# Down projections by seven products: where a pair's first half stands against the end of the pair before it

## The chip, the cores and the metric

The kernel runs on one core of one Trainium2 chip. The metric is the device time of one execution of the whole program, in microseconds (us), taken as the median of three runs. Engines are named as in the profile: PE is TensorE (matrix products), PEld its weight loads, DVE is VectorE, ACT is ScalarE, SP is SyncE, which issues the loads.

## The reference, cut to what matters

The program is a decoder trunk with two layers on 512 rows of 1024 values, all in float32. The first layer mixes tokens with a gated DeltaNet, the second with sliding-window attention on a shared K/V. Each layer ends with the same gated MLP, and the change lies in its last product only:

```python
def conv_gated_mlp(hn, w_up, conv_w, conv_b, w_down):
    u = causal_dwconv(hn @ w_up, conv_w, conv_b)
    gate, val = jnp.split(u, 2, axis=-1)
    return (jax.nn.silu(gate) * val) @ w_down

# in reference(), for each of the two layers (D_FF = 2816, D_MODEL = 1024)
h = h + conv_gated_mlp(rmsnorm(h, ffn_norm_w[layer]), ffn_w_up[layer],
                       ffn_conv_w[layer], ffn_conv_b[layer], ffn_w_down[layer])
```

## The kernel before, in words

*Layout.* Activations are kept transposed, 128 features on the partitions and the 512 rows along the free axis. A float32 operand is split into a high part (`hi`, rounded by a copy on ACT, L132) and a low part (`lo`, what the rounding left, a subtraction on DVE, L133). Each product of two operands is three matmuls: high by high, high by low, low by high (L1052, L1053 and L1054 here; L162 to L164 in the up projections).

*Up and down in two blocks.* The hidden width of 2816 is 22 tiles of 128. In each layer the kernel makes 12 tiles with an up projection and multiplies them by their rows of `w_down` (a down projection), then the other 10. That makes four down projections: layer 0 with six pairs of hidden tiles, layer 0 with five, layer 1 with six, layer 1 with five. In the profiled execution they lie at 655.7 to 718.8, 827.6 to 881.9, 1174.3 to 1237.2 and 1346.0 to 1386.6 us.

*Seven products.* The 1024 output features are eight tiles of 128, taken in four pairs (`m2` = 0 to 3). A 2 by 2 block of weights (two hidden tiles by two output tiles) times a 2 by 2 block of activations (two hidden tiles by two halves of 256 rows) is made with seven block products instead of eight. `forms()` has prepared the sums of activation blocks (`B11`, `B21`, `T1`, ...); `seven_products()` makes the sums of weight blocks on DVE and runs the products. In the last down projection the last pair of output tiles is done plainly (`last_mm`) and goes with the final normalisation.

*Steps of a pair.* `seven_products` is a generator. Its `yield`s cut a pair into three steps:
- first half (`u` = 0): the products `a` (B11), `b` (B21), `d` (T1) and `c` (T4) over the first three pairs of hidden tiles; 36 matmuls.
- second half (`u` = 1): the same over the remaining two or three pairs, after which DVE adds the four sums to `h`.
- end: T2 and B22 are added up in the banks of `a` and `d` (a `cast` for each half); the block A22 of both halves is rounded into `w4` (`cast_to`, L156 on DVE); DVE adds `a` and `d` to `h`; then the products T3 run from `w4` into `e`, which DVE adds to `h` last. 54 matmuls with six pairs.

*What sets the order.* The order in which the generators are advanced, `(0, 1, 0, 0, 1, 1)` for pairs 0 and 1 and three steps in a row for each later pair, is the order in which the instructions are written down. Below that a scheduler places the instructions on each engine by its own estimates of when operands are ready, so neighbours on DVE can change places. Each engine then runs its list strictly in order and waits by semaphores.

*Weight buffers.* The weights of each half (`sts[u]`, 768 KB for three pairs of hidden tiles) are loaded by SP in `down_stage` (L1034). Two loads of three take a buffer of the tag `stage`, every third one the buffer `st3`; there are three buffers in all. So load number n takes the buffer of load n - 3, and can be issued once that has been read for the last time. For the load of a second half, that is the buffer of the first half of the pair before, whose last reader is the first `cast_to` in that pair's end. DVE also writes the weight sums into these buffers in place (L1063, L1071, L1072, L1080). `whi` and `wlo` have three buffers each, in `cast` and `weights`.

*Banks.* Sums are held in banks of tags `d`, `g`, `s` and `p`: `a` in `d`, `b` in `g`, the product `d` in `s`, `c` in `p` for even pairs and `d` for odd ones, `e` in `g` for even pairs and `p` for odd ones.

## Time and profile before

| what | value |
|---|---|
| times of the three runs | 1419.02, 1417.68, 1416.81 us |
| median | 1417.68 us |
| span of the profiled execution | 1412.6 us (the profile gives no other time of it) |
| busy: PE, PEld | 1384.7 (98%), 1167.1 us (83%) |
| busy: DVE, ACT | 1108.1 (78%), 748.1 us (53%) |
| the four down projections, by the stretches above | 63.1, 54.3, 62.9 and 40.6 us |

The profile is of one execution. A row of the busy times by stretch has the stretch (start:end, in us from the start of the span), its length, and then, for PE, weight loads, DVE, ACT, POOL and SP in this order, the busy time and in brackets the number of instructions; behind them the mean granted TensorE clock (1.00 is full), the busy share of the DMA engines and the GB/s moved. A row of the chain of waits has the start, the time the chain spends there, the engine, what is written (and, of a load, from what) and the line. A row of a timeline has the start, the duration, the engine, the line, the operation, output<-inputs, its size, and in brackets the idle time ahead of it with what ended it. SPq stands for the issue of a DMA on SP's queue.

### The profile page before, as it was taken

The numbers are of one execution on the slowest core, as the hardware profiler recorded it, in microseconds if no ns is written. First come the engines' busy times: TensorE is split into PE (matmuls) and PEld (weight loads), VectorE is DVE, ScalarE is ACT, GpSimd is POOL, SyncE is SP. The second block draws the span as 40 slices with busy tenths as digits, with TensorE's granted clock in tenths as the row PEclk, the third lists the DMA queues.
The fourth block names the chain that finished last, engine by engine and source line by source line (L and its number), as shares of the span: only waits on it lengthen the run. The fifth ranks groups of instructions, "written<-read, shape, count | busy, mean of one in ns | idle before, by whom it ended". The sixth has DMA issues, their size and how long they took to land.

```text
span 1412.6 us, 21751 instructions
## 1 busy us (share of the span) xinstructions
PE 1384.7 (98%) x8370; PEld 1167.1 (83%) x8370; DVE 1108.1 (78%) x2070; ACT 748.1 (53%) x1470; POOL 15.6 (1%) x37
## 2 busy tenths in 40 slices
PE   7999999999999999999999999999999999999998
PEld 5787888878877888888988889777788888988897
DVE  4996896978856438879878889788668888878996
ACT  7764566656658225444344446567544444444543
POOL 1000000000100000000000000000000000000000
PEclk9999999999999999999999999999999999999999
DMA  5333254172465323221443223322132231432222
GB/s 161 92 103 115 79 175 126 61 231 84 140 225 159 119 90 112 90 90 46 135 150 119 75 79 109 109 71 76 61 112 90 90 101 49 146 106 82 92 75 75
DMA packets 162299, 151.80 MB, mean 107 GB/s; under 512 B 24148, under 2 KB 150677, under 8 KB 162197
## 3 DMA queue, kind: packets, MB, share of 16 engines
q1 hardware_dynamic: 159938, 150.22, 33.2%
q8 instruction: 66, 1.08, 0.3%
q10 hardware_dynamic: 2259, 0.20, 0.1%
q14 instruction: 36, 0.29, 0.1%
HBM read 133.60 MB, written 15.75 MB: 106 GB/s over the span
## 4 chain that ended last, share of the span: by engine, by line
PE 87%; DVE 6%; DMA 2%; ACT 2%; issue 1%; SPq 0%; DVEq 0%; ACTq 0%
PE d L162 20%; PE d L163 20%; PE d L164 20%; PE g L198 2%; DVE wlo L133 2%; PE d L1054 1%; PE d L1207 1%; PE d L1211 1%; PE d L1209 1%; PE d L1052 1%; PE d L1053 1%; PE s L1054 1%; PE s L1052 1%; PE s L1053 1%; PE s L659 1%
## 5 line engine op out<-in xcount | busy, mean ns | idle before, releaser
L162 PE MATMUL d<-xh,whi 128*128 128x512 f32 x1128 | 444.2, 394 | 0.2
L163 PE MATMUL d<-xl,whi 128*128 128x512 f32 x1128 | 444.0, 394 | 0.0
L164 PE MATMUL d<-xh,wlo 128*128 128x512 f32 x1128 | 441.9, 393 | 0.3 <-DVE wlo L156 0.3
L132 ACT CAST whi<-stage 128x1024 fp32r<-128x1024 f32 (+2 forms) x234 | 227.4, 976 | 247.7 <-PE d L163 165.1
L133 DVE TENSOR_TENSOR wlo<-stage,whi 128x1024 fp32r<-128x1024 f32 (+2 forms) x234 | 263.4, 1128 | 70.4 <-ACT whi L132 69.6
L162 PEld LDWEIGHTS d<-xh,whi 128*128 128x128 f32 x1128 | 211.7, 188 | 44.9 <-ACT xh L172 0.5
L164 PEld LDWEIGHTS d<-xh,wlo 128*128 128x128 f32 x1128 | 211.6, 188 | 44.6 <-DVE wlo L156 0.7
L163 PEld LDWEIGHTS d<-xl,whi 128*128 128x128 f32 x1128 | 211.7, 188 | 43.2 <-issue 0.5
L280 DVE SCALAR_TENSOR_TENSOR acc<-d,cwc,acc 128x511 f32<-128x511 f32 (+2 forms) x96 | 70.7, 739 | 8.7 <-ACT acc L277 7.9
L913 DVE TENSOR_TENSOR sz<-d,p6s 128x512 f32<-128x512 f32 x59 | 40.6, 688 | 42.9 <-PE d L164 40.7
L935 ACT ACTIVATE dt<-dt 128x512 f32<-128x512 f32 x44 | 27.8, 631 | 78.3 <-DVE dt L918 78.3
L918 DVE SCALAR_TENSOR_TENSOR dt<-sz,fcw,dt 128x511 f32<-128x511 f32 (+1 forms) x60 | 44.8, 747 | 1.8 <-ACT dt L916 0.9
L918 DVE SCALAR_TENSOR_TENSOR va<-sz,fcw,va 128x511 f32<-128x511 f32 (+1 forms) x58 | 43.3, 747 | 0.9
L561 DVE TENSOR_TENSOR sT<-sT,p6s 64x31 f32<-64x31 f32 (+15 forms) x124 | 40.9, 330 | 2.0
L555 DVE TENSOR_TENSOR p6s<-sN,sT 64x31 f32<-64x31 f32 (+15 forms) x124 | 40.7, 328 | 1.9
L1276 ACT ACTIVATE dt<-dt,sm 128x256 f32<-128x256 f32 (+1 forms) x64 | 30.1, 471 | 21.5 <-DVE sm L1259 21.5
L132 ACT CAST whi<-st 128x768 fp32r<-128x768 f32 (+1 forms) x30 | 23.7, 792 | 30.5 <-PE g L1053 9.0
L913 DVE TENSOR_TENSOR zl<-d,p6s 128x512 f32<-128x512 f32 x29 | 20.0, 688 | 17.8 <-PE d L164 17.8
L682 ACT ACTIVATE rq<-o 128x128 f32<-128x128 f32 x64 | 19.0, 301 | 25.4 <-DVE o L677 22.3
L937 DVE TENSOR_TENSOR va<-dt,va 128x512 f32<-128x512 f32 x44 | 30.4, 690 | 1.2
L133 DVE TENSOR_TENSOR wlo<-st,whi 128x768 fp32r<-128x768 f32 (+1 forms) x30 | 26.8, 899 | 2.2 <-ACT whi L132 2.2
L916 ACT ACTIVATE dt<-sz,normc,fcw 128x512 f32<-128x512 f32 x30 | 24.5, 815 | 6.5 <-DVE sz L913 6.0
(770 smaller groups left out, 2876.2 us busy)
## 6 DMA issues: line engine op xcount, KB each, us to landing
stage<-in_ffn_w_up_dram SPq DMA_DIRECT2D x44, 1024.0 KB, 4.8
stage<-in_a_w_in_dram SPq DMA_DIRECT2D x23, 1024.0 KB, 5.8
stage<-in_ffn_w_down_dram SPq DMA_DIRECT2D x16, 768.0 KB, 4.3
stage<-in_a_w_out_dram SPq DMA_DIRECT2D x8, 1024.0 KB, 5.0
st<-in_ffn_w_down_dram SPq DMA_DIRECT2D x8, 768.0 KB, 5.3
zd<-sz SPq DMA_DIRECT2D x16, 256.0 KB, 2.6
od<-o SPq DMA_DIRECT2D x16, 256.0 KB
stage<-in_b_w_q_dram SPq DMA_DIRECT2D x4, 1024.0 KB, 5.0
```

The costliest lines, as they stand in the source:

```text
L132: S.copy(hi[:, :kt, :m], src)
L133: V.tensor_tensor(lo[:, :kt, :m], src, hi[:, :kt, :m].bitcast(F32), op=ALU.subtract)
L162: PE.matmul(ps, hi[:, k, :m], xh[k], start=first and k == 0, stop=False)
L163: PE.matmul(ps, hi[:, k, :m], xl[k][:], start=False, stop=False)
L164: done.append(PE.matmul(ps, lo[:, k, :m], xh[k], start=False, stop=last and k == kt - 1))
L280: V.scalar_tensor_tensor(acc[:, d:], ps[:, : T - d], col, acc[:, d:], op0=ALU.mult, op1=ALU.add)
L555: V.tensor_tensor(tv, N[:, s, s + 1 : 32].unsqueeze(2).to_broadcast([64, n, m]), Tm[:, s : s + 1, 0:m].to_broadcast([64, n, m]), op=ALU.mult,)
L561: V.tensor_tensor(Tm[:, s + 1 : 32, 0:m], Tm[:, s + 1 : 32, 0:m], tv, op=ALU.subtract)
L913: V.tensor_tensor(u[:], ps[:], rs[:], op=ALU.mult)
L918: V.scalar_tensor_tensor(acc[:, d:], u[:, : T - d], tap(2 - d, t), acc[:, d:], op0=ALU.mult, op1=ALU.add)
L937: V.tensor_tensor(b[:], a[:], b[:], op=ALU.mult)
L1276: S.activation(ej, ej, AF.Exp, bias=ngm[:, i : i + 1], scale=-1.0, accum_out=den[:, i : i + 1])
```

## The change

The order of the steps changes; in pairs (m2) and steps (first half F, second half S, end E):

```
before   0F 1F 0S 0E 1S 1E 2F 2S 2E 3F 3S 3E
after    0F 1F 0S 0E 1S 2F 1E 2S 3F 2E 3S 3E
last down projection (three pairs by seven products)
before   0F 1F 0S 0E 1S 1E 2F 2S 2E
after    0F 1F 0S 0E 1S 2F 1E 2S 2E
```

The first half of pair 1 stands where it stood. The first halves of pairs 2 and 3 now stand ahead of the end of the pair before. The sum `e` takes a bank of tag `g` in all pairs. No instruction is added or dropped, and SP issues the loads in the same order as before.

```diff
--- before.py
+++ after.py
@@ -945,14 +945,14 @@
                 sts = [down_stage(src) for src in srcs]
                 if not (plain and m2 == KD // 2 - 1):
                     todo.append(seven_products(sts, srcs, parts, sevens, h_pairs[m2], m2 % 2))
-
                     if m2 == 1:
-                        for i in (0, 1, 0, 0, 1, 1):
-                            next(todo[i])
+                        advance(todo, "0 1 0")
                     elif m2 > 1:
-                        for _ in range(3):
-                            next(todo[m2])
+                        advance(todo, f"{m2 - 2} {m2 - 1} {m2} ")
+                    if m2 == KD // 2 - 1:
+                        advance(todo, f"{m2 - 1} {m2} {m2}")
                     continue
+                advance(todo, f"{m2 - 2} {m2 - 1} {m2 - 1}")
                 xs2 = [x for f in sevens for x in (f["f0"], f["f1"])]
 
                 def last_mm(ps, ws, ts, u):
@@ -1021,6 +1021,10 @@
         out.update(halves(("T1", "T2"), parts(ta[:], next(rows), next(rows))))
         out.update(halves(("T3", "T4"), parts(tb[:], next(rows), next(rows))))
         return out
+
+    def advance(todo, order):
+        for i in order.split():
+            next(todo[int(i)])
 
     turns = [0]
 
@@ -1079,7 +1083,7 @@
                 add(h21, c)
             V.tensor_tensor(A22, A22, A11, op=ALU.subtract)
             yield
-        e = bank("p" if odd else "g")[:, 0:256]
+        e = bank("g")[:, 0:256]
         w4 = weights()
         for u in range(2):
             w = cast(sts[u], 2 * len(parts[u]), 0)
```

In the changed kernel the lines from the new function on are numbered four higher: L1052 to L1054 become L1056 to L1058, L1057 becomes L1061, L1063 L1067, L1071 L1075, L1072 L1076, L1080 L1084.

The lists of DVE in the first down projection show the three places that the prediction speaks of. `h4` and `pz` are output tiles, into which a sum of a bank (`d`, `g`, `s`, `p`) is added; `stage` and `st3` are weight buffers, in which weight sums are made in place; `whi` and `wlo` are the high and low parts.

The first place is DVE behind the last read of the buffer that the load for pair 2's second half takes. Before (the first row is that read, from `st3_995`; the first use of the load, into `st3_1036`, stands two rows behind the last one shown):

```order
L156 TENSOR_TENSOR wlo_1030_6469<-st3_995_6183,whi_1029_6468 128x384
L1057 TENSOR_TENSOR h4_4550<-h4_4550,d_1008_6242 128x256
L156 TENSOR_TENSOR wlo_1030_6469<-stage_996_6185,whi_1029_6468 128x384
L133 TENSOR_TENSOR wlo_1034_6495<-stage_996_6185,whi_1033_6494 128x768
L1063 TENSOR_TENSOR stage_1035_6539<-stage_1035_6539 128x3x128
L133 TENSOR_TENSOR wlo_1042_6549<-stage_1035_6539,whi_1041_6548 128x768
L1057 TENSOR_TENSOR h4_4550<-h4_4550,d_1005_6239 128x768
L1071 TENSOR_TENSOR stage_1035_6539<-stage_1035_6539 128x3x128
L1057 TENSOR_TENSOR h4_4550<-h4_4550,s_1007_6241 128x256
L1072 TENSOR_TENSOR stage_1035_6539<-stage_1035_6539 128x3x128
L133 TENSOR_TENSOR wlo_1044_6573<-stage_1035_6539,whi_1043_6572 128x768
L1057 TENSOR_TENSOR h4_4550<-h4_4550,p_1028_6467 128x512
```

After (the first row is the read, the last one the first use of the load, now called `st3_1018`):

```order
L156 TENSOR_TENSOR wlo_1042_6529<-st3_995_6183,whi_1041_6528 128x384
L156 TENSOR_TENSOR wlo_1042_6529<-stage_996_6185,whi_1041_6528 128x384
L133 TENSOR_TENSOR wlo_1046_6555<-stage_996_6185,whi_1045_6554 128x768
L1061 TENSOR_TENSOR h4_4550<-h4_4550,d_1005_6239 128x768
L1061 TENSOR_TENSOR h4_4550<-h4_4550,s_1007_6241 128x256
L1067 TENSOR_TENSOR st3_1018_6345<-st3_1018_6345 128x3x128
```

Before, the sums and casts of a whole first half (`stage_1035`) stand between the two; now only the rest of pair 1's end stands there, two low parts and two additions.

The second place is what follows on DVE. Before, from that first use on, with pair 3's first half in `stage_1056`:

```order
L1063 TENSOR_TENSOR st3_1036_6541<-st3_1036_6541 128x3x128
L133 TENSOR_TENSOR wlo_1046_6597<-st3_1036_6541,whi_1045_6596 128x768
L1063 TENSOR_TENSOR stage_1056_6719<-stage_1056_6719 128x3x128
L1071 TENSOR_TENSOR st3_1036_6541<-st3_1036_6541 128x3x128
L133 TENSOR_TENSOR wlo_1048_6623<-st3_1036_6541,whi_1047_6622 128x768
```

After, with pair 3's first half in `stage_1038`:

```order
L1067 TENSOR_TENSOR st3_1018_6345<-st3_1018_6345 128x3x128
L133 TENSOR_TENSOR wlo_1048_6601<-st3_1018_6345,whi_1047_6600 128x768
L133 TENSOR_TENSOR wlo_1050_6627<-st3_1018_6345,whi_1049_6626 128x768
L1061 TENSOR_TENSOR h4_4550<-h4_4550,g_1040_6527 128x512
L1061 TENSOR_TENSOR pz_728_4551<-pz_728_4551,d_1030_6471 128x256
L1075 TENSOR_TENSOR st3_1018_6345<-st3_1018_6345 128x3x128
L1061 TENSOR_TENSOR pz_728_4551<-pz_728_4551,g_1031_6472 128x256
L1076 TENSOR_TENSOR st3_1018_6345<-st3_1018_6345 128x3x128
L1084 TENSOR_TENSOR st3_1018_6345<-st3_1018_6345 128x3x128
L1061 TENSOR_TENSOR pz_728_4551<-pz_728_4551,s_1032_6473 128x256
L1067 TENSOR_TENSOR stage_1038_6523<-stage_1038_6523 128x3x128
L1061 TENSOR_TENSOR pz_728_4551<-pz_728_4551,p_1033_6474 128x256
```

The first weight sum of pair 3's first half (L1063 on `stage_1056`, now L1067 on `stage_1038`), which the second of its two casts reads, stood two rows behind; now it stands ten rows behind, after two low parts, the last addition of pair 1 (`h4` from `g_1040`), three additions of pair 2 (`pz_728`) and three weight sums.

The third place is the end of the first down projection, where the next up projection's first weights (`stage_1077`) are split. Before:

```order
L1057 TENSOR_TENSOR pz_729_4552<-pz_729_4552,d_1058_6723 128x768
L1057 TENSOR_TENSOR pz_729_4552<-pz_729_4552,s_1060_6725 128x256
L133 TENSOR_TENSOR wlo_1080_6904<-stage_1077_6899,whi_1079_6903 128x1024
L1057 TENSOR_TENSOR pz_729_4552<-pz_729_4552,p_1070_6827 128x512
L133 TENSOR_TENSOR wlo_1085_6940<-stage_1078_6901,whi_1084_6939 128x1024
```

After:

```order
L1061 TENSOR_TENSOR pz_729_4552<-pz_729_4552,d_1051_6651 128x768
L1061 TENSOR_TENSOR pz_729_4552<-pz_729_4552,s_1053_6653 128x256
L1061 TENSOR_TENSOR pz_729_4552<-pz_729_4552,g_1070_6827 128x512
L133 TENSOR_TENSOR wlo_1080_6904<-stage_1077_6899,whi_1079_6903 128x1024
L133 TENSOR_TENSOR wlo_1085_6940<-stage_1078_6901,whi_1084_6939 128x1024
```

The addition of pair 3's `e` (`p_1070` before, `g_1070` now) and the low part from `stage_1077` have changed places.

## The prediction

> I call the four down projections D1 to D4 in the order in which they run, the pairs of output tiles 0 to 3 (`m2`), and the three steps of a pair H0, H1 and E (first half, second half, end). All times are microseconds (us).

> **What bounds the kernel now.** I read the page first, then the busy times by stage, then the chain of waits, then the two queues that feed these stages.

> ```profile
> PE 1384.7 (98%) x8370; PEld 1167.1 (83%) x8370; DVE 1108.1 (78%) x2070; ACT 748.1 (53%) x1470; POOL 15.6 (1%) x37
> PE 87%; DVE 6%; DMA 2%; ACT 2%; issue 1%; SPq 0%; DVEq 0%; ACTq 0%
> stage<-in_ffn_w_down_dram SPq DMA_DIRECT2D x16, 768.0 KB, 4.3
> ```

> TensorE (PE) bounds the program: 98% of the span and 87% of the chain. So the change can only win what TensorE stands still in D1 to D4. The busy times of D1 to D4, in this order, with the number of matmuls in brackets behind each:

> ```profile
> 655.70:718.80 63.10, 61.96 (x506) 60.84 (x505) 55.76 (x96) 25.81 (x36) 0.00 (x0) 1.00 0.35 114
> 827.60:881.90 54.30, 52.16 (x422) 50.80 (x421) 51.52 (x100) 29.98 (x52) 0.00 (x0) 1.00 0.31 94
> 1174.30:1237.20 62.90, 61.95 (x506) 60.87 (x506) 56.08 (x95) 26.86 (x37) 0.00 (x0) 1.00 0.34 109
> 1346.00:1386.60 40.60, 39.38 (x319) 38.36 (x318) 38.61 (x76) 19.90 (x32) 0.00 (x0) 1.00 0.24 78
> ```

> A matmul of these stages starts 0.12 after the one before it (below: 676.77, 676.89). 1753 of them are 210.4 of the 220.9 us, so TensorE stands still for about 10.5 us in all four. Where it does is seen from the same columns from pair 1's H1 onward, the only part whose order is new. Rows are D1 in three pieces, then D2, D3 and D4:

> ```profile
> 676.40:688.50 12.10, 11.67 (x90) 11.06 (x91) 11.51 (x21) 4.97 (x7) 0.00 (x0) 1.00 0.41 137
> 688.50:703.60 15.10, 15.10 (x128) 15.10 (x127) 13.55 (x25) 5.93 (x8) 0.00 (x0) 1.00 0.34 111
> 703.60:718.80 15.20, 15.20 (x129) 15.20 (x128) 12.54 (x21) 5.32 (x7) 0.00 (x0) 1.00 0.50 161
> 846.80:868.90 22.10, 21.74 (x175) 21.19 (x176) 22.00 (x43) 13.80 (x22) 0.00 (x0) 1.00 0.35 111
> 868.90:882.00 13.10, 12.97 (x108) 12.77 (x107) 12.90 (x26) 7.54 (x17) 0.00 (x0) 1.00 0.31 97
> 1194.80:1222.00 27.20, 26.78 (x216) 26.17 (x217) 25.08 (x44) 10.89 (x15) 0.00 (x0) 1.00 0.41 134
> 1364.40:1386.60 22.20, 22.00 (x179) 21.41 (x178) 22.07 (x45) 11.51 (x19) 0.00 (x0) 1.00 0.32 107
> ```

> In pairs 2 and 3 of D1 (688.5 to 718.8) TensorE is never idle, and the weight loads beside it (second busy column) are as full. The reader should also see VectorE (third column): in D1 and D3 it has about 10% spare, in D2 and D4 none (22.00 of 22.10, 22.07 of 22.20).

> [...]

> The pauses have one model, the place where H1 follows an E directly. Today that is pair 1's H1 behind pair 0's E. In the chain of waits and on TensorE in D1:

> ```profile
> 670.35 0.48 DVE wlo L156
> 670.85 4.59 DMA stage<-in_ffn_w_down_dram
> 675.54 0.85 ACT whi L132
> 669.32 0.28 PE L1052 MATMUL d<-qT,whi 128*128 128x256 f32 x1
> 675.80 0.28 PE L1054 MATMUL g<-m,wlo 128*128 128x256 f32 x1
> 676.43 0.39 PE L1052 MATMUL d<-at,whi 128*128 128x256 f32 x1 [0.35 <-ACT whi L132]
> 676.77 0.28 PE L1052 MATMUL g<-at,whi 128*128 128x256 f32 x1
> 676.89 0.28 PE L1053 MATMUL g<-at,whi 128*128 128x256 f32 x1
> ```

> E reads the pair's weights for the last time at L156; only then may the weights for the next pair's H1 be loaded into that buffer. From 670.83 to 676.43 is 5.6: 4.59 for the load, 0.85 for the cast, the rest hand-over. TensorE had E to do meanwhile, 54 matmuls or 6.48, but L156 ended 1.5 after E's first matmul (669.32), so 0.5 was missing. VectorE then ran late too: 12.10 for 90 matmuls (10.8) is another 1.3. **Such a place costs about 1.8 in D1.** The same subtraction in the rows of the other stages gives 22.10 - 175 x 0.12 = 1.1 for D2, 27.20 - 216 x 0.12 = 1.3 for D3 and 22.20 - 179 x 0.12 = 0.7 for D4. Those windows begin with the late start, but how much of it lies ahead of them I can't read there, so I add D1's 0.5 to each: at most 1.6, 1.8 and 1.2.

> **The change part by part.** No matmul, cast, addition or load is added or dropped; SP issues the same loads in the same order. What moves is pair 2's and pair 3's H0, each ahead of the E of the pair before. Pair 1's H0 stays. This puts H1 directly behind an E at two new places in D1, D2 and D3 (pairs 2 and 3) and one in D4 (pair 2): seven. Also, e is always in a g bank; that moves nothing in time unless the two g banks run out, and each new b or e follows the addition that frees its bank by at least one H0 of other work. I cost it at nothing.

> *The loads for H1.* Today H0 stands between, and the load has this lead (SP's queue, then TensorE's first matmul of pair 2's H1):

> ```profile
> 682.85 0.37 SPq L1034 DMA_DIRECT2D st<-in_ffn_w_down_dram  x1
> 692.83 0.28 PE L1052 MATMUL d<-at,whi 128*128 128x256 f32 x1
> 696.55 0.37 SPq L1034 DMA_DIRECT2D stage<-in_ffn_w_down_dram  x1
> 697.15 0.28 PE L1052 MATMUL d<-qT,whi 128*128 128x256 f32 x1
> ```

> Issue to need is 9.98, of which 5.6 are used. Taking H0 (36 matmuls, 4.32) out leaves 5.66: just enough. What decides is how far VectorE is ahead of TensorE when E begins: in pair 2's E it was 0.6 ahead (L156 done at 696.55, E from 697.15), in pair 0's E 1.5 behind. With VectorE now held up at each landing I take 0.4 behind: 6.48 - 0.4 - 5.6 leaves 0.5 to spare, so H1 starts on time. The bounds are the two cases seen: 0.6 ahead would leave 6.48 + 0.6 - 5.6 = 1.5 to spare, 1.5 behind would miss H1 by 0.6.

> [...]

> *VectorE behind the landing, D1 and D3.* VectorE stands in order, and the additions and casts of H1 and then of pair 3's H0 all queue behind the landing. Their prices:

> ```profile
> 676.41 0.96 DVE L133 TENSOR_TENSOR wlo<-stage,whi 128x768 fp32r<-128x768 f32 x1 [0.39 <-ACT whi L132]
> 689.29 0.68 DVE L1057 TENSOR_TENSOR h<-h,p 128x512 f32<-128x512 f32 x1
> 689.89 0.55 DVE L1080 TENSOR_TENSOR stage<-stage 128x384 f32<-128x384 f32 x1
> 690.36 0.55 DVE L1063 TENSOR_TENSOR st<-st 128x384 f32<-128x384 f32 x1
> 690.83 0.95 DVE L133 TENSOR_TENSOR wlo<-st,whi 128x768 fp32r<-128x768 f32 x1
> 691.70 0.55 DVE L1063 TENSOR_TENSOR stage<-stage 128x384 f32<-128x384 f32 x1
> 694.44 0.41 DVE L1057 TENSOR_TENSOR pz<-pz,d 128x256 f32<-128x256 f32 x1
> 694.77 0.95 DVE L133 TENSOR_TENSOR wlo<-stage,whi 128x768 fp32r<-128x768 f32 x1
> ```

> Start to start that is 0.60 (e into two tiles), 0.47 (384 wide), 0.87 (low part, 768), 0.33 (256 wide). After the landing (675.44) the first low part starts at +0.97 and TensorE at +0.99. The new order then has: two low parts 1.74, e 0.60, three sums into pair 2's tiles 0.99, three weight combinations 1.41, and last the addition that pair 3's second cast needs, 0.55: it ends at +6.26. The cast adds 0.05 + 0.83, hand-over 0.05: TensorE gets it at +7.2. TensorE needs it after 36 matmuls of H1 and 4 of H0, at +0.99 + 4.8 = +5.8, later by the 0.5 to spare: +6.3. Loss 0.9 each in D1 and D3, **1.8 together** (bounds 0 with 1.4 or more to spare, and 1.4 plus a late H1 of 0.6, or 2.0, each).

> *The end of D1.* In the new order VectorE adds pair 3's e first and only then makes the low part of the next up projection's weights; before, it was the other way round.

> ```profile
> 717.66 1.23 DVE L133 TENSOR_TENSOR wlo<-stage,whi 128x1024 fp32r<-128x1024 f32 x1 [0.45 <-ACT whi L132]
> 718.95 0.69 DVE L1057 TENSOR_TENSOR pz<-pz,p 128x512 f32<-128x512 f32 x1
> 718.63 0.28 PE L1054 MATMUL p<-m,wlo 128*128 128x256 f32 x1
> 719.22 0.39 PE L164 MATMUL d<-xh,wlo 128*128 128x512 f32 x1
> ```

> The addition starts 0.32 after the last matmul; 0.32 + 0.60 + 1.23 + 0.05 is 2.2, and the third matmul of the up projection, now 0.59 after it, needs that low part: **1.6**. That load's lead also shrinks, but its delay lies inside these 1.6. Bounds: 0, which needs TensorE's last matmul some 2 earlier against the next weights' landing, so that the sum is there before the low part's input; and 2.2. Behind D3 the first low part stays ahead of e and only the second falls behind it; behind D2 one small cast for the K and V weights moves ahead of e. I cost both at nothing: TensorE has a whole chunk of other matmuls between.

> *D2 and D4.* VectorE has no spare there and its work is the same, so what is lost is what its order costs TensorE. Bounds: below 0, since VectorE's total does not grow and a better order could even win; above, each new place at its highest price, 2 x 1.6 and 1.2. I take 0.9 for D2, rather more than half of one place: its two places come one behind the other, and a VectorE that is busy throughout can be put off by the first only until the second. For D4 with its one place I take half, 0.6. Both lie nearer to the low end, because the row that speaks for the high one (pair 0's E, 1.5 behind) has VectorE still at the up projection's work.

> **Sum**: 1.8 + 1.6 + 0.9 + 0.6 = 4.9 on the profiled span of 1412.6. The profile lists no time beside that span; the median of the three runs shown, 1417.7, is 5.1 above it, and I take that as what lies around. 1412.6 + 4.9 + 5.1 = **1422.6 us**.

> **The rivals.** *Every new place costs what the old one does*: 2 x 1.8 + 2 x 1.6 + 2 x 1.8 + 1.2 = 11.6, so 1429.3. For it: same buffers, same loads, same 5.6 against 6.48. Against: pair 0's E begins with VectorE still busy with the up projection's tail, the later ones do not.

> *The cover holds* (or the move does little): VectorE stays 0.6 ahead of E, H1 has 1.5 to spare, and only the end of D1 costs: 1417.7 to 1419.3. For it: D1's 10% spare on VectorE. Against: the order above, in which 4 VectorE instructions stand between release and next use where 12 stood.

> *Faster.* TensorE's pauses in pair 1's H1, for a low part, might be filled by pair 2's H0, whose 36 matmuls are now there:

> ```profile
> 680.06 0.28 PE L1053 MATMUL p<-nt,whi 128*128 128x256 f32 x1
> 680.74 0.39 PE L1054 MATMUL s<-ktok,wlo 128*128 128x256 f32 x1 [0.40 <-DVE wlo L133]
> ```

> With everything filled from pair 1's H1 on, that is 1.3 in D1, 1.1 in D2 and 13.10 - 108 x 0.12 = 0.1 at its end, 1.3 in D3 and 0.7 in D4: 4.5 as an upper end, 1413.2. It decides if enough of the matmuls stand ahead of the waiting one; but the new order puts four there, as many as the old (with other names).

> **How the numbers follow.** A measurement here can tell about 0.2%, 2.8 us. Forecast (some 3 to 7.5 lost) 0.60; every place at full price 0.16; cover holds 0.18; faster 0.06. Slower by over 0.2% is the first two, 0.76; within it 0.18; faster 0.06. The range leaves out most of the fastest case and the top of the dearest: 1418.3 to 1427.8; the forecast's own is 1420.5 to 1425.2.

> **What would show it.** In D1 and D3: pair 2's H1 starts without a pause while its load lands under 2 before, and about 0.9 is lost in pair 3's H0 behind an ACT cast. Behind D1: the third up matmul waits for the low part, behind the sum of e. In D2 and D4: new short pauses for `whi` and `wlo`, and no more VectorE work. Wrong if H1 itself waits for the load (dearer), if loads land later now that two overlap, or if pauses of pair 1's H1 vanish.

## The result

| | before | with the change |
|---|---|---|
| median of six runs each | 1417.24 us | 1425.81 us |
| lowest to highest | 1414.51 to 1422.04 | 1421.13 to 1428.52 |
| span of the profiled execution | 1412.6 us | 1426.7 us |

The ratio is 1.006 with a 95% interval of 1.004 to 1.008: the change costs 5.7 to 11.3 us. 1422.6 was forecast, in a range of 1418.3 to 1427.8. The direction and the range held; the forecast's 4.9 of loss were 8.6 by the medians.

The profiled execution of the changed kernel has a time of its own, 1428.52, 1.8 above its span. It is the slowest of its six, and by the same 1.8 the profiled execution of before took about 1414.4, as little as the quickest of its six (1414.51). So the two traces lie 14.1 apart where the medians lie 8.6 apart. They are good for where the time goes; for how much of it goes in a usual execution, the other runs' traces are needed too.

**The profile after.** From the page: the engines, the chain of waits, and the first product of the up projections, which now waits for a cast (4.1 us in all; the page of before has 0.2 in the same row, the last one shown).

```profile
PE 1388.8 (97%) x8370; PEld 1170.9 (82%) x8370; DVE 1108.3 (78%) x2070; ACT 746.5 (52%) x1470; POOL 14.6 (1%) x37
PE 81%; DVE 8%; DMA 6%; ACT 3%; issue 1%; SPq 0%; DVEq 0%; ACTq 0%
L162 PE MATMUL d<-xh,whi 128*128 128x512 f32 x1128 | 445.9, 396 | 4.1 <-ACT whi L132 4.0
L162 PE MATMUL d<-xh,whi 128*128 128x512 f32 x1128 | 444.2, 394 | 0.2
```

VectorE's and ScalarE's work is what it was; the chain has 6% of loads where it had 2%. Busy times by stretch, with the same columns as before: D1, the pause behind it, the start of the up projection after that pause and what follows, then D2, D3 and D4.

```profile
657.40:721.50 64.10, 62.14 (x505) 60.88 (x504) 54.88 (x95) 24.58 (x35) 0.00 (x0) 1.00 0.31 96
721.50:725.60 4.10, 0.18 (x2) 0.00 (x0) 0.69 (x1) 1.04 (x1) 0.00 (x0) 0.88 1.05 368
725.60:731.40 5.80, 5.72 (x13) 4.07 (x14) 3.58 (x3) 1.99 (x2) 0.00 (x0) 0.50 0.14 48
731.40:735.00 3.60, 3.60 (x17) 2.97 (x16) 0.66 (x1) 0.88 (x1) 0.00 (x0) 1.00 0.83 284
837.50:894.20 56.70, 53.47 (x422) 51.10 (x421) 53.46 (x103) 30.41 (x54) 0.00 (x0) 1.00 0.29 90
1185.10:1248.90 63.80, 61.93 (x505) 60.81 (x504) 55.58 (x95) 25.75 (x37) 0.00 (x0) 1.00 0.30 98
1357.80:1401.00 43.20, 40.16 (x322) 38.78 (x321) 39.53 (x77) 19.86 (x32) 0.00 (x0) 1.00 0.23 74
```

TensorE stood still for 4.1 us behind D1, and for the 5.8 after that its granted clock was 0.50. Who waits for the loads of `w_down` says it shortest. Before, by the view of their issuing line (microseconds, times):

```profile
  ACT whi L132: 15.7, 4
```

After:

```profile
  ACT whi L132: 41.4, 15
```

ScalarE's casts waited 4 times for a load of this line; now 15 times. (Not every wait of ScalarE holds up TensorE.)

The next table puts the kernels side by side. Lengths go from the first matmul of a stage to 0.12 behind the start of its last one, by the timelines; "pause" is from there to the first up matmul, "up" the time from the first to the 49th up matmul behind it, "rest" from the end of D4 to the end. All in us, of one profiled execution each; the other kernels are those of the experiments below.

| kernel | D1 | pause | up | D2 | D3 | D4 | rest |
|---|---|---|---|---|---|---|---|
| before | 63.03 | 0.00 | 10.91 | 54.32 | 62.79 | 40.56 | 26.12 |
| changed | 64.07 | 4.13 | 13.93 | 56.64 | 63.82 | 43.25 | 25.67 |
| pair2_only | 63.07 | 0.00 | 11.79 | 55.76 | 63.07 | 43.06 | 25.66 |
| d1_pair3_old | 63.50 | 0.07 | 11.83 | 56.85 | 63.87 | 42.97 | 25.69 |
| d1_d3_only | 63.77 | 1.86 | 13.40 | 53.81 | 63.87 | 40.55 | 26.13 |
| d4_half_load | 63.71 | 0.88 | 11.82 | 56.71 | 63.83 | 42.29 | 25.34 |
| serial_up | 64.09 | 1.80 | 13.39 | 56.70 | 63.70 | 42.99 | 25.34 |
| old_order_g | 63.25 | 0.00 | 10.91 | 54.03 | 62.87 | 40.55 | 26.14 |
| late_up2 | 62.87 | 1.04 | 11.84 | 53.65 | 62.71 | 40.56 | 25.78 |
| late_up3 | 63.03 | 6.31 | 12.82 | 54.24 | 62.71 | 40.65 | 25.78 |
| no_overlap | 62.68 | 0.00 | 10.91 | 54.77 | 62.68 | 40.80 | 26.01 |

Where the program of a stage is the same, its length agrees within 0.4, but for the old order's D2 (53.65 to 54.32). Of the changed kernel's losses, 1.5 come back in the stretch between D2 and D3 (292.46 before, 290.97 now; why is not shown) and 0.45 behind D4, so D2 costs 2.3 - 1.5 = 0.8 net and D4 2.7 - 0.45 = 2.2. Summed over the table the changed kernel's execution lost 12.3 in these places; 1.7 of the 14.1 between the two spans lay ahead of D1, where the kernels are the same.

Executions differ by more than that where the program is the same: D1 began at 655.7 in the execution of before, at 662.0 in that of `d1_d3_only`. TensorE's granted clock can differ too: here are the same 8 us of the two, far ahead of D1, with 1.00 and 0.79.

```profile
425.00:433.00 8.00, 8.00 (x54) 7.19 (x52) 5.41 (x14) 5.88 (x18) 0.00 (x0) 1.00 0.51 169
425.00:433.00 8.00, 5.95 (x31) 5.39 (x31) 3.73 (x11) 4.02 (x9) 0.00 (x0) 0.79 0.70 227
```

So a difference of one or two us between two medians of a few executions says little here, and the places in the table say more.

**The end of D1**, in the chain of waits of the changed kernel:

```profile
704.13 4.66 DMA stage<-in_ffn_w_down_dram
...
715.78 0.48 DVE wlo L156
716.27 8.18 DMA stage<-in_ffn_w_up_dram
724.55 1.05 ACT whi L132
725.65 0.80 PE d L162
726.45 0.43 PE d L163
```

Before, the same read of the buffer, VectorE's first L156 in pair 3's end, and the issue behind it stood here:

```profile
710.81 0.55 DVE L156 TENSOR_TENSOR wlo<-stage,whi 128x384 fp32r<-128x384 f32 x1
711.39 0.37 SPq L122 DMA_DIRECT2D stage<-in_ffn_w_up_dram  x1
```

D1 ended at 718.75 then, 7.4 behind the issue; now it ended at 721.51, 5.2 behind it. The load for pair 3's H1 had landed at 708.79 (first row), so VectorE, with all it had queued behind that landing, came 2 us later to L156. The load, issued with 2.1 us less of lead, took 8.18 in this execution, where the one before had landed within 5.2.

**Inside D4 and D2** a moved H0 waits for its own load. In the changed kernel's timelines of SP, ScalarE and TensorE, first D4 (pair 2), then D2 (pair 3), each with the issue, the cast and the first matmul of H0:

```profile
1372.80 0.37 SPq L1038 DMA_DIRECT2D stage<-in_ffn_w_down_dram  x1
1379.13 0.83 ACT L132 CAST whi<-stage 128x768 fp32r<-128x768 f32 x1 [0.89 <-DMA stage<-in_ffn_w_down_dram]
1380.01 0.39 PE L1056 MATMUL d<-ktok,whi 128*128 128x256 f32 x1 [1.29 <-ACT whi L132]
866.98 0.37 SPq L1038 DMA_DIRECT2D st<-in_ffn_w_down_dram  x1
872.93 0.83 ACT L132 CAST whi<-st 128x768 fp32r<-128x768 f32 x1 [0.97 <-DMA st<-in_ffn_w_down_dram]
873.81 0.39 PE L1056 MATMUL d<-qT,whi 128*128 128x256 f32 x1 [0.93 <-ACT whi L132]
```

**Inside D1 and D3** pair 3's H0 pauses before its fifth matmul, whose cast waits for VectorE's sum. The cast and the matmul, first in D1, then in D3:

```profile
699.31 0.83 ACT L132 CAST whi<-stage 128x768 fp32r<-128x768 f32 x1 [2.15 <-DVE stage L1067]
700.20 0.39 PE L1056 MATMUL s<-qT,whi 128*128 128x256 f32 x1 [0.56 <-ACT whi L132]
1226.82 0.83 ACT L132 CAST whi<-stage 128x768 fp32r<-128x768 f32 x1 [2.62 <-DVE stage L1067]
1227.71 0.39 PE L1056 MATMUL s<-ktok,whi 128*128 128x256 f32 x1 [0.56 <-ACT whi L132]
```

The pitch there says more than the idle time, since the matmuls overlap (rows of 0.28 start 0.12 apart): in D1 from 699.36 to 700.20 is 0.84, 0.72 over the usual 0.12.

### The profile page after: what moved, and what is told of

It is laid out like the page before. It is cut to its first block, busy times and chain, and to the rows that moved or that the text cites. A ratio compares the mean times of both kernels' runs of the same rounds, so it can differ in the third digit from the quotient of the medians.

```text
span 1426.7 us, 21746 instructions
## 1 busy us (share of the span) xinstructions
PE 1388.8 (97%) x8370; PEld 1170.9 (82%) x8370; DVE 1108.3 (78%) x2070; ACT 746.5 (52%) x1470; POOL 14.6 (1%) x37
## 4 chain that ended last, share of the span: by engine, by line
PE 81%; DVE 8%; DMA 6%; ACT 3%; issue 1%; SPq 0%; DVEq 0%; ACTq 0%
PE d L162 20%; PE d L163 20%; PE d L164 20%; DVE wlo L133 3%; DMA stage<-in_ffn_w_down_dram 2%; PE g L198 2%; PE d L1211 1%; PE d L1215 1%; PE d L1213 1%; ACT whi L132 1%; DMA st<-in_ffn_w_down_dram 1%; PE s L659 1%; PE p L1307 1%; PE g L1291 1%; PE s L651 1%
## 5 line engine op out<-in xcount | busy, mean ns | idle before, releaser
L164 PE MATMUL d<-xh,wlo 128*128 128x512 f32 x1128 | 443.0, 394 | 0.0
L132 ACT CAST whi<-stage 128x1024 fp32r<-128x1024 f32 (+2 forms) x234 | 227.1, 975 | 258.6 <-PE d L163 165.8
L133 DVE TENSOR_TENSOR wlo<-stage,whi 128x1024 fp32r<-128x1024 f32 (+2 forms) x234 | 262.9, 1128 | 71.2 <-ACT whi L132 70.3
L164 PEld LDWEIGHTS d<-xh,wlo 128*128 128x128 f32 x1128 | 212.2, 188 | 44.6 <-DVE wlo L133 0.8
L132 ACT CAST whi<-st 128x768 fp32r<-128x768 f32 (+1 forms) x30 | 23.4, 790 | 31.8 <-DMA st<-in_ffn_w_down_dram 10.9
L133 DVE TENSOR_TENSOR wlo<-st,whi 128x768 fp32r<-128x768 f32 (+1 forms) x30 | 26.6, 899 | 1.7 <-ACT whi L132 1.6
## 6 DMA issues: line engine op xcount, KB each, us to landing
stage<-in_ffn_w_down_dram SPq DMA_DIRECT2D x16, 768.0 KB, 4.2
st<-in_ffn_w_down_dram SPq DMA_DIRECT2D x8, 768.0 KB, 7.0
```

The costliest lines, as they stand in the source:

```text
L132: S.copy(hi[:, :kt, :m], src)
L133: V.tensor_tensor(lo[:, :kt, :m], src, hi[:, :kt, :m].bitcast(F32), op=ALU.subtract)
L164: done.append(PE.matmul(ps, lo[:, k, :m], xh[k], start=False, stop=last and k == kt - 1))
```

## Experiments

In each diff `steps` gives, for `m2` = 0 to 3, the order in which the generators are advanced. The diffs show the lines that matter; `...` stands for other lines in between. Each ratio is to the kernel before, run in the same round, where its median lay between 1415.4 and 1417.2. Where a kernel has these tables, e takes a g bank in all pairs, as in the changed kernel.

### Undo one pair, or two projections

`d1_pair3_old`, in D1 alone:

```diff
-steps = ["", "0 1 0", "0 1 2", "1 2 3 2 3 3"]
+steps = ["", "0 1 0", "0 1 2", "1 2 2 3 3 3"]
```

> The changed kernel, but in D1 (layer 0, six pairs of hidden tiles) pair 3's first half is back behind pair 2's end; D2 to D4 as changed. Theory A, from the changed kernel's trace: the order of D1's last pair makes the first load of the next up projection late (VectorE frees its buffer only 5.2 us ahead of D1's end, and it shares the DMA engines with the second load), which costs a pause of 4.1, some 2.6 of half clock behind it and 0.7 in pair 3's first half. Then this kernel is 6.5 to 7.5 us faster than the changed one (1425.8): 1418.3 to 1419.3, with under 0.5 of a pause between D1 and the up projection. Theory B, from the prediction: the end of D1 costs 1.6 by the order of the e addition and the low part on VectorE, and the load only comes on top; here that order is back too, so B says 1.6 + 0.9 = 2.5 less: 1423.3.

Measured: 1423.29, ratio to before 1.0046 (1.0031 to 1.006). The pause behind D1 is gone (0.07) and so is the half clock (the up matmuls start 0.23 apart again); 0.9 stays in the up projection, since the first low part is waited for once. VectorE makes that low part ahead of e again (by the rows below), so the order of the two does not make this wait: the load, issued 7.1 ahead of D1's end, took 6.1 where the one before took 5.2, and the cast that the low part needs came that much later.

```profile
722.47 1.23 DVE L139 TENSOR_TENSOR wlo<-stage,whi 128x1024 fp32r<-128x1024 f32 x1 [1.59 <-ACT whi L138]
723.61 0.68 DVE L1062 TENSOR_TENSOR pz<-pz,g 128x512 f32<-128x512 f32 x1
```

By the trace this place went from 7.2 to 1.0. By the medians the kernel is only 2.5 faster than the changed one, which is the size that theory B gave, and not theory A's 6.5 to 7.5. B's mechanism is not borne out all the same (the rows of the changed kernel under "Why the prediction was right or wrong", and `late_up2` below); A's size I took from an execution in which this place was at its dearest. The table has two more executions with D1 exactly as changed: they lose 1.9 + 2.5 = 4.4 (`d1_d3_only`) and 0.9 + 0.9 = 1.8 (`d4_half_load`) behind D1.

`d1_d3_only`, in D2 and D4:

```diff
-steps = ["", "0 1 0", "0 1 2", "1 2 2" if plain else "1 2 3 2 3 3"]
+steps = ["", "0 1 0 0 1 1", "2 2 2", "" if plain else "3 3 3"]
```

> The new order in D1 and D3 (six pairs of hidden tiles) alone; D2 and D4 (five pairs) with the old order. By the traces D2 lost 2.3 us inside (1.5 of it given back behind it) and D4 2.1, so this kernel should be 2.5 to 4.5 us faster than the changed one: 1421.3 to 1423.3. If what D2 and D4 lost was no more than the prediction gave them (0.9 and 0.6) it is 1.5 faster: 1424.3.

Measured: 1423.42, ratio 1.0045 (1.0029 to 1.006): 2.4 below the changed kernel, between the two expectations (1.5, and 2.5 to 4.5). The stages themselves are clear: D2 is 2.8 and D4 2.7 shorter than in the changed kernel, and all of D1 and D3 stays. It also says that D1 and D3 with the end of D1 are dearer than the prediction had them: 6.4 by this ratio (4.1 to 8.5), where it gave them 1.8 + 1.6.

`pair2_only`, in all four:

```diff
-steps = ["", "0 1 0", "0 1 2", "1 2 2" if plain else "1 2 3 2 3 3"]
+steps = ["", "0 1 0", "0 1 2", "1 2 2" if plain else "1 2 2 3 3 3"]
```

> In all four projections only pair 2's first half is moved ahead of pair 1's end; pair 3's stands behind pair 2's end as before. Theory: the price is paid by each moved first half for itself, so D2 loses about half of 2.4 (55.3 to 55.7 long), D1 and D3 0.3 to 0.6 (63.1 to 63.6), D4 as in the changed kernel 2.4 to 2.7, and behind D1 at most 1. Sum 3.5 to 5 slower than before: 1420.4 to 1422. If the second moved half pays for the first as well (as I argued for D2), D2 is no longer than 54.6.

Measured: 1419.74, ratio 1.0028 (1.0017 to 1.0039), about 4 us: as expected. D1 is as long as before, so pair 2's H1 does start on time there, right behind pair 1's E; D3 loses 0.3, D2 1.4 (a little over half), D4 2.5. What pair 3's move adds is 0.9 in D2, 0.8 to 1.0 each in D1 and D3, and the rest of the end of D1, where this kernel loses 0.9.

### The up projection's load behind D1

`serial_up`: in the changed kernel the second of the two up loads waits for the first.

```diff
+        if behind is not None:
+            G.tensor_copy(st[:, 0, 0:1], behind[:, 0, 0:1])
...
-                sv = load_stage(wup, 0, 8, DFF + t * P)
+                sv = load_stage(wup, 0, 8, DFF + t * P, sg if (l, t) == (0, 12) else None)
```

> The changed kernel, but the second load of the up projection behind D1 starts only when the first has landed (a one-column copy on GpSimd from the first into the second's buffer stands ahead of it). Theory A, sharing: the first load took 8.2 us because two loads of 1 MB ran at once; alone, or with only the small K/V loads beside it, it takes 5.2 to 6.2, the pause falls from 4.1 to 1 to 2, TensorE keeps its clock, and the kernel is 4 to 5.5 us faster than the changed one: 1420.3 to 1421.8. If the load's late issue alone makes the pause, the first load still takes about 8 and the time stays at 1425.8; if the second load is then missed in its turn, a new pause shows some 5.5 us into the up projection.

Measured: 1424.55, ratio 1.005 (1.0037 to 1.0063), 1.3 below the changed kernel and not told apart from it. The first load, without the second beside it, landed and was cast 6.1 behind its issue. With the second beside it this took 8.3 in the changed kernel's execution, 6.1 in `d1_d3_only`, 5.1 in `d4_half_load` and 5.2 in the next run. So sharing between the two loads does not explain the 8.18: it was a slow execution of this load, and what made it slow stays open. The pause of 1.8 with a load of normal length is the part that the late issue makes.

`keep_clock`: the changed kernel with idle matmuls behind D1.

```diff
+                        if (l, t0) == (0, 0):
+                            x = sevens[5]["T3"][0]
+                            ps = bank("p")[:, 0:256]
+                            for _ in range(30):
+                                PE.matmul(ps, x[:, 0:P], x, start=True, stop=True)
```

> The changed kernel with 30 matmuls more, whose sums nobody reads, written behind D1's last product: 26 of them fall into the pause ahead of the up projection (about 3.1 us), 4 into pair 3's first half (0.5). Theory: the matmuls behind the pause ran at half the clock because TensorE stood still for 4 us. Then the pause (end of D1 to the first up matmul) stays at 4.1, but the up projection's matmuls start at 0.23 apart instead of 0.43 and the kernel is 2 to 2.6 us faster than the changed one: 1423.2 to 1423.8. Rival: they were slow for another reason (their weights or their operands came late): the first 12 stay at 0.43 apart and the time at 1425.8 or a little above.

Measured: 1423.77, ratio 1.0046 (1.0032 to 1.006). TensorE was busy throughout, and its clock stayed at 1.00 in the row of the stretch behind D1:

```profile
720.50:723.70 3.20, 3.20 (x29) 3.20 (x28) 1.91 (x2) 0.89 (x1) 0.00 (x0) 1.00 1.08 374
723.70:729.00 5.30, 5.30 (x25) 4.38 (x25) 2.36 (x2) 2.00 (x2) 0.00 (x0) 1.00 0.29 98
```

But in this execution the load came after 5.2 and TensorE would have stood still for no more than 1 us and then 0.8, which did not cost it the clock in `late_up2` below (1.04 and then 0.80, clock 1.00). So the expected time came out, and proves little by itself.

To see the load's lateness alone, the next kernels change nothing but this load, in the kernel before. `late_up` exchanged the two tiles that are allocated for the two loads:

```diff
+                if (l, t) == (0, 12):
+                    sv, sg = [wpool.tile([P, 8, 256], F32, tag="stage", bufs=2, name=nm("stage")) for _ in range(2)]
...
```

> The kernel before (old order, old banks), with one thing changed: behind D1 the two first loads of the next up projection exchange their buffers, so that the first of them takes the buffer that is freed second and is issued 4.5 us ahead of D1's end instead of 7.4 (in the changed kernel 5.2 to 5.4). Theory A: this load's lateness alone makes the cost at D1's end, with its two parts, TensorE's pause and the half clock behind it. Landing 5.1 to 6 after issue and cast 1.05, less 4.5, gives a pause of 1.7 to 2.6, then some 0.8 for the first low part and 1.8 of half clock: 4 to 5 us slower than before, 1421 to 1422, with a granted clock of about 0.5 to 0.6 in some 3.6 us behind the pause. Theory B (the order of e's addition and the low part on VectorE makes it): that order is the old one here, so no more than 1 slower, and TensorE's clock stays at 1.00.

Measured: 1415.86, ratio 1.0 (0.9989 to 1.0011). Both loads were issued when they had been before, 7.4 and 4.5 ahead of D1's end: the buffer seems to go to the tile that is written first, not to the one allocated first. So the load's lateness was not tried here. `late_up2` holds the load back by data instead:

```diff
+            G.tensor_copy(st[:, 0, 0:1], behind[:, 6, 0:1].bitcast(F32))
...
-                sg = load_stage(wup, 0, 8, t * P)
+                sg = load_stage(wup, 0, 8, t * P, last_w4[0][1] if (l, t) == (0, 12) else None)
```

> The kernel before, in which the first load of the up projection behind D1 may start only when the last low part of D1's weights has been written (a one-column copy on GpSimd stands ahead of it): issued about 4.4 us ahead of D1's end instead of 7.4; in the changed kernel it was 5.2 to 5.4. The order on TensorE, VectorE, ScalarE and SyncE is that of before. (In the earlier try with exchanged buffers the loads kept their times, -7.4 and -4.5, so it tried nothing.) Theory A, lateness of this load alone: landing 5.1 to 6 after issue, cast 1.05, less 4.4, a pause of 1.7 to 2.7, 0.8 for the first low part, and half clock (matmuls 0.43 apart) for some 3.6 behind it, 1.8: 4 to 5 slower than before. Theory B, the order of e's addition and the low part: that is the old one, so under 1 slower.

Measured: 1419.18, ratio 1.002 (1.0011 to 1.0029), 1.6 to 4.1 slower, with VectorE's order that of before. The load was issued 6.1 ahead of D1's end (the low part that it waits for, that of pair 3's second half, came earlier than I had read). It landed and was cast in 6.1; the pause is 1.04, the first low part is waited for another 0.8, and the clock stays:

```profile
722.80:725.20 2.40, 0.99 (x5) 0.35 (x4) 1.33 (x2) 1.04 (x1) 0.00 (x0) 1.00 1.05 347
725.20:730.20 5.00, 5.00 (x22) 4.13 (x23) 2.85 (x3) 2.00 (x2) 0.00 (x0) 1.00 0.27 93
```

So 1.3 us less of lead for this one load, which took 0.9 longer in this execution than in that of before, costs about 2 in the trace. Theory B gave under 1.

`late_up2_keep` adds 18 idle matmuls to it, written like those of `keep_clock`.

> The same with 18 matmuls (2.16 us), whose sums nobody reads, behind D1's last product. If the half clock comes from TensorE's standing still, the up projection's matmuls now start 0.23 apart at once, and the kernel is about 1.8 us faster than the one with the late load alone; the start of the first up matmul moves by no more than 0.5. If the half clock has another cause it is as long as without them.

Measured: 1418.56, ratio 1.0022 (1.0013 to 1.003). The idle matmuls came behind the first five up matmuls, so they filled nothing, and there was no half clock to remove (1.00 in all rows from 720 to 732). It tells nothing on what halves the clock.

`late_up3` doubles the dose, with a later value to wait for:

```diff
-            G.tensor_copy(st[:, 0, 0:1], behind[:, 6, 0:1].bitcast(F32))
+            G.tensor_copy(st[:, 0, 0:1], behind[:, 0, 256:257])
...
-                sg = load_stage(wup, 0, 8, t * P, last_w4[0][1] if (l, t) == (0, 12) else None)
+                sg = load_stage(wup, 0, 8, t * P, h_pairs[3] if (l, t) == (0, 12) else None)
```

> As the run with the late load, but the first load of the up projection behind D1 now waits for the last but one addition into pair 3's tiles: issued about 1.4 us ahead of D1's end (7.4 before, 6.1 in the run with the late load). All else is the kernel before, but for the addition of e, which comes ahead of the first low part, and two of the small K/V loads, which come ahead of this load. With 1.04 + 0.80 of standing still TensorE kept its clock, with 1.80 + 0.81 and with 4.1 it lost half of it. If standing still is what halves the clock, independent of the order of steps, then here a pause of 4.7 to 5.7 and 0.8 more is followed by matmuls 0.43 apart for 5 to 6 us (2.4 lost): 8 to 9 us slower than before. If the clock stays at 1.00 behind this pause the half clock came from something else in the new order, and it is 5.5 to 6.5 slower.

Measured: 1423.77, ratio 1.0051 (1.0037 to 1.0065), 5.2 to 9.2 slower; the trace has 6.31 of pause and 1.9 in the 48 up matmuls behind it, 8.2 in all. The three stretches (pause, behind it, later) and the chain of waits:

```profile
719.40:725.70 6.30, 0.18 (x2) 0.00 (x0) 0.69 (x1) 1.04 (x1) 0.00 (x0) 0.73 1.01 344
725.70:729.20 3.50, 3.42 (x7) 2.31 (x8) 1.97 (x2) 1.82 (x2) 0.00 (x0) 0.51 0.31 111
729.20:735.00 5.80, 5.80 (x27) 4.76 (x26) 3.13 (x4) 1.94 (x3) 0.00 (x0) 1.00 0.52 171
```

```profile
718.31 6.24 DMA stage<-in_ffn_w_up_dram
724.64 1.05 ACT whi L134
725.74 0.80 PE d L164
726.53 0.43 PE d L165
```

In the old order of steps, with the old order of products, the pause of 6.31 brings the half clock with it (0.51): that is shown. It lasted 3.5 us behind the pause, less than the 5 to 6 expected, and had begun inside the pause, whose mean clock is 0.73.

### D4: the moved half's own load

`d4_half_load`: in D4, pair 2's first half loads 3 of 6 tiles. The other three are filled with zeros, so the result leaves these weights out; the work of TensorE, VectorE and ScalarE is the same.

```diff
+        if short:
+            G.memset(st[:, short:kt, :], 0.0)
+            kt = short
+        SP.dma_start(st[:, :kt, :], src[:, :kt, :])
...
+                sts = [down_stage(src, 3 if plain and m2 == 2 and i == 0 else None) for i, src in enumerate(srcs)]
```

> The changed kernel, but in D4 the load for pair 2's first half brings 3 of its 6 tiles (384 KB instead of 768); a memset on GpSimd fills the other three with zeros, so the result leaves these weights out. All work of the engines stays. Theory, from the changed kernel's trace: D4's loss of 2.7 is the lateness of this load, which in the new order is needed some 2.9 us earlier than the end of the pair ahead would allow; the pause of 1.45 in front of pair 2's first half goes, with part of the 0.54 behind it, and D4 is 41.3 to 41.8 long instead of 43.0 to 43.25. The prediction's reason (VectorE has no spare and works in a worse order): D4 stays at 43.

Measured: 1422.93, ratio 1.0045 (1.0032 to 1.0058). D4 is 42.29 long: 0.7 to 1.0 shorter than in the changed kernel and in `d1_pair3_old` and `pair2_only` (42.97 to 43.25), though not the 41.3 to 41.8 expected. The load no longer ends the wait; the cast now waits for a product of pair 1's H1 ahead of it on TensorE:

```profile
1373.92 0.84 ACT L132 CAST whi<-stage 128x768 fp32r<-128x768 f32 x1 [0.95 <-PE g L1060]
```

So the load was the last to come, by about 1 us, and behind it stands the next limit. I take that one for the buffers of `whi`, of which there are three, but no run separates it. D4 and what follows still lose 1.0 (42.29 + 25.34 against 40.56 + 26.12), of 2.2 in the changed kernel.

### The bank, and the opposite order

`old_order_g`: the old order with the change's other line.

```diff
-        e = bank("p" if odd else "g")[:, 0:256]
+        e = bank("g")[:, 0:256]
```

> The old order of steps with the change's other part alone: the sum e takes a g bank in every pair. The prediction gave this no cost: 1417 within 1. If the g banks run out, pairs 1 and 3 show new waits of products into g for an addition on VectorE, and D1 to D4 grow by some tenths each.

Measured: 1416.63, ratio 1.0002 (0.9993 to 1.0011). The bank costs nothing that can be measured, as the prediction had it.

`no_overlap`: pair 1's first half too stays behind pair 0's end.

```diff
-steps = ["", "0 1 0 0 1 1", "2 2 2", "" if plain else "3 3 3"]
+steps = ["", "0 0 0 1 1 1", "2 2 2", "" if plain else "3 3 3"]
```

> The opposite step: no pair's first half is moved, pair 1's neither, so that every pair runs first half, second half, end. If an H1 right behind an E is what costs (the price of 1.8, 1.6, 1.8 and 1.2 of the prediction, for pair 1), this kernel gains up to that: 6 us faster than before. But pair 1's first half (4.3 us) also covers pair 0's second half, whose low part arrived 0.5 late even so (0.3 in D2): without it some 3 to 5 us of pause stand there in each projection. I expect the second to win: 6 to 12 us slower than before.

Measured: 1417.17, ratio 1.0008 (0.9998 to 1.0017): neither of the two. D1 and D3 are 0.35 and 0.1 shorter, D2 and D4 0.45 and 0.24 longer. In D1 the pauses of pair 1's H1 are gone, and this one of 1.66 (669.63 to 671.41 is 1.78, the usual pitch 0.12) stands in pair 0's E instead, where before had 0.16:

```profile
671.41 0.39 PE L1059 MATMUL d<-qT,wlo 128*128 128x256 f32 x1 [1.50 <-DVE wlo L139]
```

So pair 1's H1 right behind pair 0's E, the place from which I had read the price of 1.8, can be avoided, but in D1 most of what that saves is spent in pair 0's E. No kernel here beats the kernel before.

## Why the prediction was right or wrong

- **TensorE bounds, nothing can be won but its pauses**: right. In D1 and D3 the pauses of pair 1's H1 were not filled. In D2 and D4 its wait for the low part did vanish (0.48 and 0.29 before), as the rival "faster" had it, but pauses of pair 2's H0 took its place (0.74 at its first matmul in D2, 1.45 in D4), and nothing was won. How much there was to win depends on the column that is read: in the four rows of before the pauses are 5.4 us by matmul busy time (215.5 of 220.9), 10.0 by weight loads (210.9) and 10.5 by the count of matmuls.
- **The loads for H1 arrive in time**: right. In D1 pair 2's H1 took its load 4.4 after the issue and started without a pause; `pair2_only` has D1 as long as before. None of the loads of `w_down` whose landing shows in the trace took under 4.2 in the changed kernel; the median is 4.3.
- **VectorE behind the landing, 0.9 each in D1 and D3**: right in place, cause and size. It is the fifth matmul of pair 3's H0, behind an ACT cast, 0.7 there, and 1.0 over the whole of each stage.
- **The end of D1, 1.6 by the order of e and the low part**: wrong in its mechanism, and short. The addition of e was long done when the low part's input came:

```profile
721.72 0.69 DVE L1061 TENSOR_TENSOR pz<-pz,g 128x512 f32<-128x512 f32 x1 [1.74 <-PE g L1058]
725.63 1.22 DVE L133 TENSOR_TENSOR wlo<-stage,whi 128x1024 fp32r<-128x1024 f32 x1 [3.23 <-ACT whi L132]
```

  The step that failed is the sentence that the load's delay "lies inside these 1.6". I had worked out that VectorE runs late behind the landing, and followed that to the next cast, but not on to L156, which frees the buffer of the next load. That lateness takes 2 us from the load's lead, TensorE stands still for 4.13, and in the 5.8 behind that its granted clock is 0.50. This place cost 1.8, 4.4 and 7.2 in three executions, in which the load took 5.1, 6.1 and 8.3.
- **D4, 0.6**: mis-sized; it cost 2.2 net. The step that failed is "the loads for H1": I followed only those. A moved H0 has a load too, issued in the same E 0.9 behind the load for H1, and the move takes the whole of the E (54 matmuls with six pairs of hidden tiles, fewer here) out of its lead. In D4, where H1 is only 24 matmuls, it came too late. Halving that load took away 1.2 of the 2.2 (`d4_half_load`); what makes the rest is not separated.
- **D2, 0.9**: the size came out (0.8 net), but by luck: D2 itself lost 2.3, and 1.5 came back behind it, which the prediction did not foresee. Nor was it VectorE's order alone. TensorE waited for a cast in both moved halves; pair 3's cast waited for its load (the rows above), and pair 2's stood in a row of ScalarE's other work.
- **The bank of e, nothing**: right (`old_order_g`).
- **The base**: I took the 5.1 between the profiled span and the median for what lies around a span. It is 1.8; the rest was a profiled execution quicker than the median. The sum was added to the same median either way, so the forecast does not move.

Term by term: 1.0 + 1.0 in D1 and D3 (1.8 forecast), about 4.4 in the middle execution at the end of D1 (1.6), 0.8 in D2 (0.9), 2.2 in D4 (0.6). That is 9.4, against 8.6 by the medians and 4.9 forecast. The range held through its room, not through these terms: the two that were short were each about a third of what was measured.

## What to carry to other kernels

When a step moves ahead in a pipeline of shared buffers, follow every load that it and its neighbours need, the moved step's own first: its issue hangs on the same release as before, and only its need moves. Follow a late engine past its next consumer to the next buffer that it frees, across the border of the stage. A wait can cost more than its length: in `serial_up` 2.6 us of standing still cost 4.3, because TensorE's granted clock was 0.53 in the 3.6 us behind it. So price that too.

## What the runs showed of the hardware

TensorE's clock, behind D1, by what it had stood still: 1.04 and then 0.80 us (`late_up2`), clock 1.00 afterwards; 1.80 and then 0.81 (`serial_up`), 0.53 for 3.6; 4.13 (changed kernel), 0.50 for 5.8; 6.31 (`late_up3`), 0.51 for 3.5. The row of `serial_up` behind its pause:

```profile
724.20:727.80 3.60, 3.60 (x9) 2.83 (x10) 0.00 (x0) 0.00 (x0) 0.00 (x0) 0.53 0.63 222
```

The same load of 1 MB, issued at the same point of the program (5.2 to 5.4 ahead of D1's end), had landed and its cast started 5.1, 5.2, 6.1 and 8.3 us after its issue in four executions (`d4_half_load`, `keep_clock`, `d1_d3_only`, the changed kernel). A price taken from one execution of a load would have been off by 3 us here, as much as a third of what the change cost.
